# The MLP of layer 1 as seven products of quarters in place of eight

## The chip, the cores and the metric

The kernel runs on one core of a Trainium2 chip. The metric is the time of one execution in microseconds (us) of device time. Every time here is of the whole program, both layers, unless a stretch is named.

## The reference

The reference is one inference step of a decoder trunk of two layers: a gated linear attention (GLA) layer and a differential attention layer, each followed by a squared-ReLU MLP and a layer norm over a scaled residual. There are 1024 prompt tokens, 16 meta tokens ahead of them, and 8 sample tokens of running sequences. The model width is 1024, the MLP's inner width 4096; everything is float32.

```python
def sq_relu_mlp(x, w1, w2):          # w1 (1024, 4096), w2 (4096, 1024)
    h = jax.nn.relu(x @ w1)
    return (h * h) @ w2

def post_norm(x, f, g, b):
    return layer_norm(DEEPNORM_ALPHA * x + f, g, b)
...
    # in each layer, after the attention's own post_norm
    x_p = post_norm(x_p, sq_relu_mlp(x_p, mlp_w1[layer], mlp_w2[layer]), ln_mlp_g[layer], ln_mlp_b[layer])
    x_s = post_norm(x_s, sq_relu_mlp(x_s, mlp_w1[layer], mlp_w2[layer]), ln_mlp_g[layer], ln_mlp_b[layer])
```

The change concerns `sq_relu_mlp` for layer 1, the last work of the program.

## The kernel before

**Exact products from rounded parts.** TensorE multiplies in a rounded float32 format (fp32r). To keep float32's precision each operand is held as two parts: `hi`, the rounded value, which ScalarE (ACT) writes by a copy, and `lo`, what is left, source minus `hi`. `split` (L159 to L161) does this for activations, with VectorE (DVE) as the subtractor; `unit` (L138 to L154) does it for weights, with ACT at L151 and GpSimd (POOL) at L152. `mm3` (L163 to L166) then multiplies hi by hi, hi by lo and lo by hi, so every product of a 128 x 128 block is three matmuls, and all of them show lines 164 to 166 in the profile whatever stage they belong to.

**Storage.** Activations with features on the partitions lie in `XH` and `XL`, eight blocks of 128 features by 1032 tokens (1024 prompt, 8 sample). `Y` (seen as `Yt`, eight tiles of 128 tokens by 1024) holds the residual stream with tokens on the partitions and gathers the MLP's result. Three PSUM pools share the eight banks: `mm` with three tiles (`mmt`), `ax` with three (`axt`), `sm` with two (`smt`).

**The MLP of layer 1** (`mlp`, called at L1306) takes the 4096 inner features in eight groups of 512. In each group the up map goes first: two weight operands of 256 features (`kunit`), three chunks of 344 tokens, blocks of 128 features, eight blocks of the contraction, three matmuls each. ACT applies Relu (L946) and Square (L947) in PSUM, `split` writes the result to `HH` and `HL`. Then the down map: two weight operands of 512 outputs, eight tiles of 128 tokens, four blocks of the contraction, three matmuls of 512 columns each; DVE adds the PSUM tile into `Y` (L976). The sample tokens ride in the third chunk of the up map; their down map is a few small matmuls with the unsplit weights (L967), gathered in two PSUM tiles `acc` over the whole stage. In group 0, between the up and the down map, `alpha_row` scales the residual in `Y` (L924, DVE); the matching additions (L926) are spread over groups 1 to 4. Both read a row of a parameter that is broadcast from memory into `ht`.

**Ahead of it.** `w_out` (L840) is the attention's output projection, with 256-column matmuls; `normalize` takes each finished pair of token tiles through the layer norm's statistics (L880 to L894), and `to_fm` (L900) transposes a half of 512 tokens back to features on partitions and splits it into `XH` and `XL`. The last head of the attention, with `o_fm` (L1173 to L1179), writes the projection's input.

**Behind it.** In the last group the down map is ordered so that token tiles finish one after another; `normalize` and `last` (L1262 to L1279) turn a finished tile into output. Tiles 0 to 5 go over ACT (L894), DVE (L1269) and POOL (L1272), the last two over DVE alone (L1277, L1278). `samples_out` does the same for the sample tokens.

**What sets the order.** A scheduler places each engine's instructions in a fixed order at build time, from the order of the program and a simulated timeline; each engine then takes its own queue in order. A tile pool with n buffers lets the work of n tiles be under way; a new tile waits until the oldest is released. Nearly all loads are issued on the SP queue (`dma`).

## Time and profile before

| | |
|---|---|
| time, median of 3 runs | 2965.57 us (2965.27 to 2967.11) |
| the profiled execution: time, span of its instructions | 2961.38 us, 2959.4 us |
| mean granted TensorE clock | 0.988 |
| PE busy over the span | 2848.6 us (96%) |
| DVE, ACT, POOL busy over the span | 1579.2, 944.4, 836.6 us |

The profile is of one execution, a few microseconds from the median. Engines are PE (TensorE matmuls), PEld (its weight loads, which overlap the matmuls), DVE, ACT, POOL and SP. A group's row gives line, engine, operation, tiles out<-in, shapes, count | busy us, mean ns of one | idle time of the engine just before them, and what ended it. A row of a stretch gives its length, then for each engine busy us and instructions, the granted clock of PE, the busy share of the DMA engines and GB/s. A timeline row gives start, length, engine, line, operation, tiles, form and count. A row of waits gives who waited for whom: us in total, times, longest.

### The profile page before, as it was taken

The numbers are of one execution on the slowest core, as the hardware profiler recorded it, in microseconds if no ns is written. First come the engines' busy times: TensorE is split into PE (matmuls) and PEld (weight loads), VectorE is DVE, ScalarE is ACT, GpSimd is POOL, SyncE is SP. The second block draws the span as 40 slices with busy tenths as digits, with TensorE's granted clock in tenths as the row PEclk, the third lists the DMA queues.
The fourth block names the chain that finished last, engine by engine and source line by source line (L and its number), as shares of the span: only waits on it lengthen the run. The fifth ranks groups of instructions, "written<-read, shape, count | busy, mean of one in ns | idle before, by whom it ended". The sixth has DMA issues, their size and how long they took to land.

```text
span 2959.4 us, 50682 instructions
## 1 busy us (share of the span) xinstructions
PE 2848.6 (96%) x19476; PEld 2337.9 (79%) x19476; DVE 1579.2 (53%) x2705; ACT 944.4 (32%) x1970; POOL 836.6 (28%) x605
## 2 busy tenths in 40 slices
PE   8999999999999999999999998889999999999998
PEld 5776668987777777777888887878998889888886
DVE  2664454458877777777767623779352212211115
ACT  2343354152122122123311113768252232223322
POOL 1322022234333343344223320223312222222224
PEclk9999999999999999999999999999999999999999
DMA  8667541525798898988388987563412111111111
GB/s 262 208 206 260 181 153 52 174 86 165 254 349 305 292 334 315 338 309 301 114 282 293 360 311 193 109 139 91 168 35 61 45 40 34 57 44 50 38 34 65
DMA packets 266018, 525.81 MB, mean 178 GB/s; under 512 B 30560, under 2 KB 162656, under 8 KB 261680
## 3 DMA queue, kind: packets, MB, share of 16 engines
q1 hardware_dynamic: 260736, 505.97, 50.6%
q0 software_dynamic: 5040, 16.61, 2.9%
q8 instruction: 153, 2.51, 0.3%
q14 instruction: 89, 0.73, 0.1%
HBM read 479.78 MB, written 26.12 MB: 171 GB/s over the span
## 4 chain that ended last, share of the span: by engine, by line
PE 80%; DVE 8%; DMA 7%; ACT 2%; issue 1%; POOL 1%; SPq 1%; DVEq 0%; POOLq 0%; ACTq 0%
PE mmt L164 22%; PE mmt L166 22%; PE mmt L165 22%; PE smt L780 4%; DMA XL<-XL 1%; PE smt L1159 1%; DVE pg L739 1%; PE smt L967 1%; PE smt L418 1%; DVE as L1139 1%; DVE sc L740 1%; DMA swt<-in_mlp_w 1%; DMA XH<-XH 1%; DVE Y L924 1%; PE axt L1154 1%
## 5 line engine op out<-in xcount | busy, mean ns | idle before, releaser
L152 POOL TENSOR_TENSOR wlo<-raw,whi 128x512 fp32r<-128x512 f32 x384 | 528.7, 1392 | 1350.0 <-ACT whi L151 1195.5
L164 PE MATMUL mmt<-XH,whi 128*128 128x512 f32 (+1 forms) x1536 | 556.0, 362 | 8.8 <-DVE HL L161 8.8
L166 PE MATMUL mmt<-XH,wlo 128*128 128x512 f32 (+1 forms) x1536 | 555.3, 362 | 0.0
L165 PE MATMUL mmt<-XL,whi 128*128 128x512 f32 (+1 forms) x1536 | 554.1, 361 | 0.0
L151 ACT CAST whi<-raw 128x512 fp32r<-128x512 f32 x384 | 227.7, 619 | 932.4 <-PE mmt L166 475.8
L164 PE MATMUL mmt<-whi,XH 128*128 128x256 f32 x1536 | 439.0, 287 | 10.3 <-DVE qr L1028 5.2
L166 PE MATMUL mmt<-whi,XL 128*128 128x256 f32 x1536 | 438.6, 286 | 5.4 <-DVE XL L161 5.4
L165 PE MATMUL mmt<-wlo,XH 128*128 128x256 f32 x1536 | 436.6, 285 | 0.9 <-POOL wlo L152 0.8
L164 PE MATMUL mmt<-whi,HH 128*128 128x512 f32 x1024 | 411.3, 402 | 2.0 <-DVE Y L976 2.0
L166 PE MATMUL mmt<-whi,HL 128*128 128x512 f32 x1024 | 408.5, 399 | 0.0
L165 PE MATMUL mmt<-wlo,HH 128*128 128x512 f32 x1024 | 407.3, 398 | 0.0
L740 DVE TENSOR_REDUCE sc<-pg 128x16 f32<-128x1024 f32 x256 | 309.4, 1214 | 88.6 <-POOL pg L739 85.1
L976 DVE TENSOR_TENSOR Y<-Y,mmt 128x512 f32<-128x512 f32 x256 | 174.8, 684 | 317.6 <-PE mmt L166 317.2
L164 PEld LDWEIGHTS mmt<-XH,whi 128*128 128x128 f32 x1536 | 290.8, 189 | 48.9 <-DVE HL L161 10.4
L166 PEld LDWEIGHTS mmt<-XH,wlo 128*128 128x128 f32 x1536 | 290.8, 189 | 44.4 <-issue 12.0
L165 PEld LDWEIGHTS mmt<-XL,whi 128*128 128x128 f32 x1536 | 290.9, 189 | 41.3 <-issue 8.9
L164 PEld LDWEIGHTS mmt<-whi,XH 128*128 128x128 f32 x1536 | 291.0, 190 | 25.2 <-issue 17.7
L166 PEld LDWEIGHTS mmt<-whi,XL 128*128 128x128 f32 x1536 | 291.7, 190 | 16.8 <-issue 10.5
L165 PEld LDWEIGHTS mmt<-wlo,XH 128*128 128x128 f32 x1536 | 291.2, 190 | 11.5 <-issue 9.6
L739 DVE TENSOR_TENSOR pg<-pg,qb 128x1024 f32<-128x1024 f32 x192 | 263.2, 1376 | 64.7 <-DMA pg<-in_cache_k 46.7
L161 DVE TENSOR_TENSOR HL<-mmt,HH 128x344 fp32r<-128x344 f32 (+1 forms) x160 | 92.9, 582 | 327.2 <-ACT HH L160 327.0
L164 PEld LDWEIGHTS mmt<-whi,HH 128*128 128x128 f32 x1024 | 193.2, 189 | 73.5 <-DVE Y L976 17.5
(370 smaller groups left out, 3603.4 us busy)
## 6 DMA issues: line engine op xcount, KB each, us to landing
pg<-in_cache_k SPq DMA_DIRECT2D x256, 512.0 KB
pg<-in_cache_v SPq DMA_DIRECT2D x256, 512.0 KB
raw<-in_mlp_w SPq DMA_DIRECT2D x256, 256.0 KB
swt<-in_mlp_w SPq DMA_DIRECT2D x32, 1024.0 KB
raw<-in_gla_w_in SPq DMA_DIRECT2D x48, 256.0 KB
swt<-in_gla_w_in SPq DMA_DIRECT2D x12, 1024.0 KB
swt<-in_diff_w_in SPq DMA_DIRECT2D x12, 1024.0 KB
raw<-in_diff_w_in SPq DMA_DIRECT2D x48, 256.0 KB
```

Of the source, the lines that this page charges most:

```text
L151: S.copy(hi[:, c], raw)
L152: G.tensor_tensor(lo[:, c], raw, hi[:, c].bitcast(F32), op=ALU.subtract)
L161: return eng.tensor_tensor(lo, src, hi.bitcast(F32), op=ALU.subtract)
L164: TE.matmul(ps, ah, bh, start=first, stop=False)
L165: TE.matmul(ps, ah, bl, start=False, stop=False)
L166: TE.matmul(ps, al, bh, start=False, stop=last)
L418: TE.matmul(ps[o : o + TS, :], lhs[:, k + i, :], t[:, i, c * 512 : (c + 1) * 512], start=k == 0, stop=k == nk - 2)
L739: eng.tensor_tensor(pg, pg, qb, op=ALU.mult)
L740: return V.tensor_reduce(sc[:, n, :], pg.rearrange("p (h d) -> p h d", d=64), op=ALU.add, axis=AX.X).ins
L780: m = TE.matmul(acc[i * TS : i * TS + 16, :256], w[r, n, :], pg[r, i * 256 : (i + 1) * 256], start=n == 0, stop=n == NPG).ins
L924: steps_v.append(V.scalar_tensor_tensor(y, y, ALPHA, rb, ALU.mult, ALU.mult).ins)
L976: steps_v.append(V.tensor_tensor(yv, yv, ps, op=ALU.add).ins)
```

## The change

The up map and the down map of layer 1's MLP are each cut into 2 x 2 quarters, and the four quarters of the result come from seven products of quarters rather than eight, by a form of Strassen's identity with running sums. The 4096 inner features go in four runs of 1024, each with seven products for the up map (quarters of the weights: 512 x 512; of the activations: 512 features by 516 tokens, 512 prompt and 4 sample) and seven for the down map.

- `LEFT` and `RIGHT` say what each product multiplies: a quarter, a sum or difference of two quarters, or a quarter combined with the running operand `r` (kept in `RX` for activations, `RW` for weights).
- `chip_operand` makes the operand from activations: DVE combines (if there are two terms), ACT rounds, DVE subtracts, in two halves of two blocks. `weight_operand` makes the one from weights: four blocks of 128 x 512, one or two loads each, DVE combines, ACT rounds, POOL subtracts. Both are made one product ahead, and emitted in the middle of the product before.
- `up_tile` does 12 matmuls of 258 columns and adds the result into one or two quarters of `HF` (float32, in SBUF); `hidden` applies Relu and Square there when a quarter is complete. `down_tile` does 12 matmuls of 512 columns and adds into one or two quarters of `Y`, some of them by way of `RP` and an addition on POOL.
- The input of this MLP is kept unsplit (`xr`, in the place of `XL`), so `to_fm` no longer splits it.
- Around it: `XH` and `XL` become two tiles each, one for each half of the tokens; the PSUM pools become 4, 2 and 2 tiles ahead of this layer's output projection; the last head writes all eight blocks of the first half of the tokens before its own last tiles and the second half after; the last rows to finish are token tiles 0 to 3, of which 2 and 3 go over DVE alone. `mlp` now serves layer 0 alone.

The diff, cut to its core:

```diff
+LEFT = {1: [(0, 0)], 2: [(0, 1)], 3: [(0, 1), "-r"], 4: [(1, 1)], 5: [(1, 0), "+", (1, 1)], 6: ["r-", (0, 0)], 7: [(0, 0), "-", (1, 0)]}
+RIGHT = {1: [(0, 0)], 2: [(1, 0)], 3: [(1, 1)], 4: [(1, 0), "-r"], 5: [(0, 1), "-", (0, 0)], 6: [(1, 1), "-r"], 7: [(1, 1), "-", (0, 1)]}
...
-    XH = cp.tile([P, NB, 1032], F32R, name="XH")
-    XL = cp.tile([P, NB, 1032], F32R, name="XL")
+    TH = 512 + NS // 2
+    XH = Halves([cp.tile([P, NB, TH], F32R, name="XH%d" % c, tag="XH%d" % c) for c in range(2)])
+    XL = Halves([cp.tile([P, NB, TH], F32R, name="XL%d" % c, tag="XL%d" % c) for c in range(2)])
...
+    psum(mm=4, ax=2, sm=2)
...
-    normalize(w_out(A["diff_w_out"][0], True, samples()), stats, lambda c: to_fm(c, 2))
+    normalize(w_out(A["diff_w_out"][0], True, samples()), stats, lambda c: to_fm(c, 2, xr))
...
-    normalize(mlp(1, [(0, 344), (344, 688), (688, 1032)], hs, acc, rwp, mid=samples_out), stats, lambda c: None, last)
+    def chip_operand(terms, quarter, n, tmp):
+        buf = XH.t[count[0] % 2].rearrange("p k n -> p (k n)")
+        count[0] += 1
+        hi, lo = (buf[:, i * 4 * TH : i * 4 * TH + 4 * n].rearrange("p (k n) -> p k n", n=n) for i in range(2))
+        rv, tv = (x[:, : 4 * n].rearrange("p (k n) -> p k n", n=n) for x in (RX, tmp))
+        for j in (0, 2):
+            b = slice(j, j + 2)
+            src = combine(V, terms, lambda q: quarter(*q)[:, b], rv[:, b], tv[:, b])
+            split(hi[:, b], lo[:, b], src)
+        return hi, lo
+
+    def weight_operand(i, terms, quarter, side=None):
+        hi, lo = (wsp.tile([P, 2048], F32R, name=n).rearrange("p (k n) -> p k n", n=512) for n in ("whi", "wlo"))
+        for k in range(4):
+            raws = {}
+            for q in terms:
+                if isinstance(q, tuple):
+                    w, r0, c0 = quarter(*q)
+                    count[1] += 1
+                    raws[q] = wrp.tile([P, 512], F32, name="raw") if count[1] % 7 in (0, 3) else rawt()
+                    dma(raws[q], w[r0 + k * P : r0 + (k + 1) * P, c0 : c0 + 512])
+            run = RW[:, k, :]
+            src = combine(V, terms, raws.get, run, raws[terms[0]] if i == 7 else run)
+            S.copy(hi[:, k, :], src)
+            G.tensor_tensor(lo[:, k, :], src, hi[:, k, :].bitcast(F32), op=ALU.subtract)
+            if side:
+                side(k, raws)
+        return hi, lo
...
+    def hidden(h, c, m):
+        x = HF[:, 4 * h + m, c, :]
+        S.activation(x, x, AF.Relu)
+        S.activation(x, x, AF.Square)
+        S.copy(hs[:, 4 * h + m, 4 * c : 4 * c + 4], x[:, 512:])
+
+    def up_tile(g, i, m, c, left, right, ps):
...
+        for k in range(4):
+            mm3(ps, ah[:, k, ms], al[:, k, ms], bh[:, k, cs], bl[:, k, cs], k == 0, k == 3)
...
+        if i == 1:
+            S.copy(c12, ps)
+        elif i == 2:
+            add(c11, c12, ps)
+        elif i == 5:
+            S.copy(c22, ps)
+        elif i == 6:
+            add(c21, c12, ps)
+            add(c22, c22, c21)
+        elif i == 4:
+            add(c21, c21, ps)
+        elif i == 3:
+            add(c12, c22, ps)
+        else:
+            add(c22, c22, ps)
+            add(c21, c21, ps)
+        if c:
+            for h, x in {2: [(0, 0)], 3: [(0, 1)], 7: [(1, 1), (1, 0)]}.get(i, ()):
+                hidden(h, x, m)
+
+    DOWN = {1: [(0, 0)], 6: [(0, 1)], 7: [(1, 1), (1, 0)], 4: [(1, 0)], 5: [(1, 1), (0, 1)], 3: [(0, 1)], 2: [(0, 0)]}
+
+    def down_tile(g, i, t, left, right, ps):
...
+        r = RP[:, t, :]
+        if i == 1:
+            S.copy(r, ps)
+        if i in (6, 7):
+            add(V, r, ps)
+        for c, u in DOWN[i]:
+            yv = Yt[:, 4 * c + t, 512 * u : 512 * u + 512]
+            if i in (1, 2, 3, 4, 5):
+                add(V, yv, ps)
+            else:
+                add(G, yv, r)
+
+    def mlp1():
+        seq = []
+        for g in range(4):
+            seq += [(g, 1, i) for i in (1, 2, 5, 6, 4, 3, 7)]
+            seq += [(g, 0, i) for i in ((1, 5, 6, 3, 7, 4, 2) if g < 3 else (1, 5, 6, 7, 4, 3, 2))]
+        nxt = operands(*seq[0])
+        n = 0
+        for at, (g, up, i) in enumerate(seq):
+            now = nxt
...
+            for t in range(4):
+                if t == 2 and at + 1 < len(seq):
+                    nxt = operands(*seq[at + 1])
+                if up:
+                    for c in range(2):
+                        n += 1
+                        up_tile(g, i, t, c, *now, axt() if n % 3 == 0 else mmt())
+                    continue
+                n += 1
+                down_tile(g, i, t, *now, axt() if n % 3 == 0 else mmt())
...
+    normalize(mlp1(), stats, lambda c: None, last)
```

209 lines of the change are left out of this document (134 added, 75 removed).

## The prediction

> **What bounds the kernel now.** I read the page first, then a table of stretches, then the groups of the stage that changes, then the waits of PE, then the timeline where two engines meet. The page:
>
> ```profile
> span 2959.4 us, 50682 instructions
> PE 2848.6 (96%) x19476; PEld 2337.9 (79%) x19476; DVE 1579.2 (53%) x2705; ACT 944.4 (32%) x1970; POOL 836.6 (28%) x605
> PE   8999999999999999999999998889999999999998
> ...
> PE 80%; DVE 8%; DMA 7%; ACT 2%; issue 1%; POOL 1%; SPq 1%; DVEq 0%; POOLq 0%; ACTq 0%
> ```
>
> PE is busy nearly everywhere and carries four fifths of the chain that ended last. The MLP of layer 1 runs from about 2178 us to the end, so its ten slices of 74 us are the last ten of the page. Stretches with one form of matmul each (the MLP's loop in full in the last row):
>
> ```profile
> core 0: us, PE busy (x) PEld busy (x) DVE busy (x) ACT busy (x) POOL busy (x), PEclk, DMA share, GB/s
> 532.00:580.00 48.00, 48.00 (x407) 48.00 (x408) 21.41 (x31) 7.23 (x10) 13.76 (x10) 1.00 0.45 161
> 2380.00:2420.00 40.00, 40.00 (x257) 40.00 (x256) 5.68 (x11) 17.78 (x42) 7.63 (x6) 1.00 0.08 21
> 2449.00:2470.00 21.00, 21.00 (x91) 16.92 (x90) 6.05 (x8) 1.24 (x2) 3.95 (x4) 1.00 0.24 64
> 2600.00:2700.00 100.00, 100.00 (x532) 86.95 (x530) 18.23 (x30) 27.19 (x61) 20.37 (x16) 1.00 0.14 43
> ```
>
> In the stage PE is busy 100.00 of 100 us at the full granted clock, with DVE at 18%, ACT at 27% and POOL at 20%. Dividing each stretch by its count less two (matmuls that reach over the edges) gives the pitch of a matmul: 0.1185 us for 256 columns, 0.1569 for 344 (the up map), 0.2346 for 512 (the down map). The waits of PE from 2060 us to the end are few:
>
> ```profile
> PE mmt L164 <- DVE HL L161: 3.0, 1, 3.0
> PE mmt L164 <- DVE Y L858: 0.8, 1, 0.8
> PE mmt L164 <- ACT whi L151: 0.7, 1, 0.7
> PE axt L1177 <- DVE orr L1169: 0.4, 1, 0.4
> ```
>
> So nothing but PE limits this stage, and the change takes matmuls out of it and puts vector work in.
>
> **What PE loses.** The pitch grows nearly with the columns, so 258 columns cost 0.1185 x 258/256 = 0.1194 us (an estimate; no matmul of 258 columns is in this trace). Up map: before, 8 groups x 4 blocks x 3 chunks x 8 k x 3 = 2304 matmuls of 344 columns, 2304 x 0.1569 = 361.5 us; after, 4 runs x 7 products x 8 tiles x 4 k x 3 = 2688 of 258, 320.9 us. Down map: 8 x 16 tiles x 12 = 1536 of 512, 360.3 us; after 4 x 7 x 4 x 12 = 1344, 315.3 us. Together 721.8 - 636.2 = **86 us less**. The 64 matmuls of the samples' down map stay 64.
>
> **What the vector engines gain.** Each product now needs a left and a right operand made on the chip: a sum or a difference where the identity wants one, then a rounded high part (ACT) and a remainder (DVE for the activations, POOL for the weights). Its result must be added into up to two quarters. The prices, from the stage's groups (2220 to 2900 us; those behind the dots from 2176 us on):
>
> ```profile
> L152 POOL TENSOR_TENSOR wlo<-raw,whi 128x512 fp32r<-128x512 f32 x118 | 154.4, 1328 | 554.5 <-ACT whi L151 539.8 <-ACT hs L950 10.6 <-DMA raw<-in_mlp_w 3.7
> L976 DVE TENSOR_TENSOR Y<-Y,mmt 128x512 f32<-128x512 f32 x113 | 77.7, 688 | 248.5 <-PE mmt L166 248.5
> L151 ACT CAST whi<-raw 128x512 fp32r<-128x512 f32 x118 | 69.1, 617 | 338.0 <-PE mmt L166 260.0 <-DMA raw<-in_mlp_w 55.2 <-PE mmt L165 22.7
> L967 PE MATMUL smt<-raw,hs 128*32 128x512 f32 x118 | 31.6, 605 | 0.0
> L926 DVE SCALAR_TENSOR_TENSOR Y<-ht,Y 128x1024 f32<-128x1024 f32 x8 | 9.8, 1225 | 0.3
> L950 ACT COPY hs<-mmt 128x8 f32<-128x8 f32 x31 | 5.1, 166 | 9.3 <-DVE HL L161 9.3
> ...
> L894 ACT ACTIVATE Y<-Y,brs 128x1024 f32<-128x1024 f32 x10 | 12.0, 1238 | 17.4 <-DVE brs L892 17.4
> L880 DVE BATCH_NORM_STATS2 bst<-Y 128x6 f32<-128x512 f32 x18 | 12.2, 688 | 0.3
> L1269 DVE TENSOR_TENSOR Y<-Y,pg 128x1024 f32<-128x1024 f32 x6 | 8.0, 1326 | 0.0
> L1278 DVE SCALAR_TENSOR_TENSOR Y<-Y,brs,pg 128x512 f32<-128x512 f32 x4 | 2.8, 746 | 0.4 <-POOL brs L888 0.4
> L883 DVE BATCH_NORM_AGGREGATE bmv<-bst 128x2 f32<-128x12 f32 x10 | 2.0, 203 | 0.1
> L887 DVE TENSOR_SCALAR brs<-bmv 128x1 f32<-128x1 f32 x8 | 1.2, 149 | 0.2
> ```
>
> Durations of neighbours overlap a little, so for a queue of them I take the pitch, and for what POOL and DVE do to each other the timeline, DVE's rows first (two from 700 us, one from 245 us), then POOL's from 700 us:
>
> ```profile
> 700.30 13.57 DVE L739 TENSOR_TENSOR pg<-pg,qb 128x1024 f32<-128x1024 f32 x8
> 713.80 4.59 DVE L740 TENSOR_REDUCE sc<-pg 128x16 f32<-128x1024 f32 x4
> ...
> 245.56 1.28 DVE L320 TENSOR_TENSOR t<-gb 128x512 f32<-128x512 f32 x2
> ...
> 700.44 4.47 POOL L152 TENSOR_TENSOR wlo<-raw,whi 128x512 fp32r<-128x512 f32 x2 [5.03 <-ACT whi L151]
> 706.26 4.26 POOL L152 TENSOR_TENSOR wlo<-raw,whi 128x512 fp32r<-128x512 f32 x2 [1.34 <-ACT whi L151]
> ```
>
> Alone, 1024 elements pass DVE every 1.15 us (4.59/4) and 512 every 0.64. But eight L739, which read two tiles of SBUF, took 13.57 us where four POOL subtractions of L152 lay among them: 13.57 - 8 x 1.15 = 4.4, or **1.09 us of waiting per POOL instruction**, and POOL's took 2.2 us each in place of 1.3. The two take turns; they do not share. L976 and the present L161, which read one PSUM and one SBUF tile, show no such lengthening. All the new sums, differences and remainders on DVE read two SBUF tiles.
>
> The Trainium skill, "SBUF — State Buffer", section "Who interferes with whom", speaks against this change: a DVE instruction with two SBUF inputs and a GpSimd instruction that reads SBUF exclude each other for the whole instruction. The trace agrees in kind (L739 against L152), with 1.09 us measured where the whole POOL instruction is 1.3; by the rule to the letter the lock term below would be 41 us in place of 35, and the time 2930.
>
> Per run of 1024 features, up map: DVE 14 remainders and 8 combinations of 1032 elements at 1.16, 16 combinations of weights at 0.64, 56 evictions of 258 at 0.37 (from 512 at 0.64, by size, above nothing of fixed cost; an estimate): 25.5 + 10.2 + 20.7 = 56.4 us beside PE's 672 x 0.1194 = 80.2. Down map: 22 x 1.15 + 16 x 0.64 + 32 evictions x 0.64 = 56.0 beside 78.8 and 16 sample matmuls of 0.54 (31.6 us for 59, two records each), 8.6. POOL: 28 subtractions in each map, and 12 additions into Y in the down map: 68 a run. ACT: up 28 x 0.617 + 14 x 1.24 + 16 copies at some 0.35 + 16 x (2 x 0.617 + 0.166) = 62.7, down 37. Every sum is under PE's, so **on average all of it hides**. In single products it does not. An up product lasts 96 x 0.1194 = 11.5 us, a down product 11.3 (13 to 15 with sample matmuls), and in it DVE prepares the next operand pair and evicts its own. Making products 5, 6 or 7 takes 4 x 1.15 + 4 x 0.64 = 7.2; POOL's four subtractions, if each stops DVE, 4.4. Window by window, in the order of the list:
>
> - up 2 (it makes the operands of 5): 7.2 + 3.0 of evictions + 4.4 = 14.6, 3.1 over; up 3 (those of 7) the same; up 6 (those of 4): 4.6 + 5.9 + 4.4 = 14.9, 3.4 over; up 4 (those of 3): 4.9 + 3.0 + 4.4, 0.7 over; the others none;
> - down 5 (those of 6): 7.2 + 5.1 + 4.4 = 16.7 against 13.2, 3.5 over; down 3 (those of 7): 7.2 + 2.6 + 4.4 = 14.2, 2.9 over; down 6 (those of 3): 4.6 + 2.6 + 4.4, 0.3 over; the others none.
>
> That is 17 us a run if every POOL instruction stops DVE, 0 if none does (work made ahead in the light windows included): 67 or 0 over four runs. DVE's reads of two SBUF tiles fill (38.7 + 35.5)/167.6 = 44% of a run, so about half of POOL's starts meet one: **35 us**.
>
> **The rest.** The eight L924 and eight L926 for the residual were hidden; they are two-tile reads too and now fall among a busy DVE: 16 x 1.15 = 18 us at worst, 0 at best, half taken: 9. Behind a wait of L924 for its row stand, on DVE's queue, evictions and remainders. The switch from up 7 to down 5: ACT has 4.9 us of operands and 8 x 1.4 of Relu, Square and copy in an 11.5 us window, carries 4.6 over, and the chain combine, cast, remainder adds some 4 to it; down 1 lasts 15 and covers it; uncovered it would cost up to 5 a run. Weights go up from 128 loads (half of the row of both layers below) to 288 (the SP queue, seven buffers), 75 MB in 680 us, 111 GB/s; the table has 161 GB/s at full PE speed, so 0; behind a load that waits for a buffer stand the next loads alone, mostly. The start: the 3.0 us wait on HL L161 was for the second half of the tokens; now two products (23 us) run on the first half alone: -3. The first operand's cast and remainder lie beside the last two pieces of the output projection: 0, uncovered 5. The order of the last head's transposes and the wider PSUM pool: the one wait there is 0.4, so 0, between -3 and +3.
>
> ```profile
> raw<-in_mlp_w SPq DMA_DIRECT2D x256, 256.0 KB
> ...
> 2950.49 0.68 DVE L976 TENSOR_TENSOR Y<-Y,mmt 128x512 f32<-128x512 f32 x1
> 2953.58 1.41 DVE L1278 SCALAR_TENSOR_TENSOR Y<-Y,brs,pg 128x512 f32<-128x512 f32 x2
> ```
>
> The end: rows finish every 2.8 us in the last product rather than every 5.6, and DVE has 4 x (0.69 + 0.69 + 0.35) + 2 x 1.3 + 4 x 2 x 0.75 = 15.5 us of it, which begins when the first of four tiles is done and so ends 2.8 + 15.5 - 11.3 = 7.0 after the last matmul. Before, DVE ended 4.5 after it took up the last tile (2950.49 to 2954.99). +3, between 0 and 6.
>
> The sum: -86 - 3 + 35 + 9 + 3 = -42. The profiled execution took 2961.4 us (span 2959.4), so it would take 2919; the median of the three runs lies 4.2 above it at 2965.6, and on that scale the forecast is **2924 us**.
>
> **The rivals.** *All of it hides* (chance 0.18): the combinations are made ahead in the light windows and POOL falls between DVE's PSUM reads. For it: DVE's mean load of 112/168. Against: L739 and L152 met in turn whenever both had work. -86 - 3 + 3: 2880. *Operands come late* (0.20, the other side): engines take their queues in order, so an eviction that waits for PE stands ahead of a combination that PE's next product waits for. Then each of 55 products after the first starts late by one locked pair, 2.24 us (4.47/2): 123 - 86 + 9 = 46 slower, 3012. It decides against the change from 1.4 us a product on. For it: the locked pairs are real, and one operand is four links of combine, cast and subtract. Against: casts of L151 now start as soon as PE frees a buffer (260.0 us of their idle time ended so), so work is already ordered well ahead. *The smaller tile does not get cheaper* (0.03): were 258 columns to cost what 344 do, the up map would take 2688 x 0.1569 = 421.8, and 60 + 41 are lost: 101 - 42, 3025. The stretch at 532 us speaks against it. *In between* (0.09): late by 1.0 to 1.6 us a product, 2950 to 2985.
>
> **How the numbers follow.** The forecast, with overruns between 15 and 60 us, has 0.50. Range: from 2888, which leaves about half of the all-hidden case below, to 2985, which leaves the late case's upper part and the small-tile case above. A measurement of this kernel tells about 0.2%, 6 us, from no change. Faster by more: 0.50 + 0.18 + a little of the in-between, 0.71. Within: 0.05. Slower: 0.20 + 0.03 + the rest of the in-between, 0.24. The forecast's own range is 2900 to 2948.
>
> **What would show it.** Right: PE at 92 to 96% in the stage, DVE near 75 to 90%, POOL's L152 with a mean of 1.5 to 2.0 us, PE's waits led by DVE remainders and POOL's wlo at products 5, 6 and 7, a matmul of 258 columns at a pitch near 0.119. Wrong: PE at 99% (all hides); waits of equal size at every product (late operands); PE's waits led by ACT or by loads; a pitch over 0.13.

## The result, and the profile after

The change made the kernel slower: 2978.58 us (median; 2974.21 to 2986.99) against 2967.11 us before (2960.8 to 2975.4), measured on the same chip, a ratio of 1.0040 with a 95% interval of 1.0026 to 1.0055. I had forecast 2924, with 2888 to 2985 as the range: the time lies inside it, but the change went the other way than the one to which I gave 0.71, some 12 us slower by the ratio.

The profiled execution has a span of 2980.0 us, 20.6 more than before. The same lines of its page as were shown of before:

```profile
span 2980.0 us, 52275 instructions
PE 2799.5 (94%) x19668; PEld 2285.8 (77%) x19668; DVE 2013.0 (68%) x3122; ACT 1076.7 (36%) x2113; POOL 1147.2 (38%) x749
PE   8899999999999999999899998898998999999995
...
PE 25%; DVE 11%; DMA 5%; POOL 4%; issue 4%; ACT 1%; SPq 0%; DVEq 0%; POOLq 0%; ACTq 0%
```

PE is 49 us less busy in a longer span. The chain that ended last can't be set beside the one of before: followed back from the end it breaks off at 1476 us, so its shares add up to 50% where those of before add up to 99%. In the half that was followed PE has half, and VectorE, loads and GpSimd most of the rest. Stretches of the MLP (length, then busy us and instructions of PE, PEld, DVE, ACT, POOL, granted clock, DMA share, GB/s); the first row is the whole MLP before the change, the others are of after: the whole MLP, an up product 6 (18.4 us where 11.5 is undisturbed), a down product 7 (19.2 where 12.3 is), and the last product but one (33.6 where 11.1 is):

```profile
2178.00:2946.00 768.00, 765.00 (x4021) 660.06 (x4021) 191.78 (x314) 217.92 (x471) 184.36 (x153) 1.00 0.15 44
```

```profile
2201.00:2961.00 760.00, 699.04 (x4216) 603.12 (x4214) 626.30 (x733) 350.34 (x619) 485.34 (x292) 0.95 0.31 101
2436.10:2454.60 18.50, 14.21 (x99) 14.01 (x98) 16.65 (x18) 5.05 (x8) 8.50 (x5) 0.82 0.40 129
2538.30:2557.50 19.20, 16.10 (x57) 10.60 (x56) 14.75 (x14) 5.64 (x8) 16.79 (x11) 0.82 0.33 110
2913.50:2947.10 33.60, 15.38 (x67) 10.80 (x64) 25.12 (x45) 8.26 (x11) 25.88 (x26) 0.78 0.21 80
```

(Products are named by their map and number; runs 0 to 3 are the four runs of 1024 inner features.) Three things are to be seen. The MLP itself takes 760 us in place of 768: nearly all that PE was to save is gone. PE stands idle for 61 us of it (760.00 - 699.04; 3 before). And the granted clock has a mean of 0.95 where it was 1.00: with a clock of 1.0 or 0.5 that makes some 76 us at half speed. In the products that lost most both come together; up product 2 of run 0 (16.8 us) and up products 6 and 4 of run 3 (13.7 and 14.5) lost their 2 to 5 us at the full clock.

The 20.6 us by place, from the starts of the same matmuls in both traces: the first transposes of the attention come 2.4 earlier by chance (the instructions up to there are the same); from there to the MLP's first matmul 375.2 us in place of 349.6, so **25.5 more before the MLP begins** (five runs below leave the program unchanged up to there, and in them this stretch took 367.3 to 375.1 us, so single executions differ by some 8 us here); the MLP 8.4 less; from its last matmul to the end 18.8 in place of 13.0, 5.8 more.

In the MLP, each of the 56 products can be read off by its first matmul. Undisturbed they last 11.5 us (up), 11.1 (down), 14.35, 12.33 and 12.31 (down 1, 5 and 7, with sample matmuls), 656 in all; 104 us are lost, in four places of about equal size: up products 1, 2, 5, 6 and 4 of run 0 (25), down product 7 of every run (27), up products 6 and their neighbours in runs 1 to 3 (26), and the last two products of all (26). What PE waited for, from 2201 us to the end (in total, times, longest):

```profile
PE mmt L191 <- DVE HF L1414: 11.6, 8, 4.3
PE mmt L192 <- POOL wlo L1379: 9.9, 9, 2.0
PE smt L474 <- DVE ss L472: 7.7, 1, 7.7
PE mmt L192 <- DVE XH L188: 6.8, 2, 5.8
PE axt L191 <- DVE HF L1414: 5.9, 4, 2.9
PE smt L1333 <- DVE sx L487: 5.6, 1, 5.6
```

They are PSUM tiles that VectorE has not emptied (L1414), weight remainders of GpSimd (L1379), remainders of the activations that VectorE makes (L188), and the samples' small chain (L474, L1333), which no part of the prediction counted.

### The profile page after: what moved, and what is told of

Read it like the earlier page. It is cut to its first block, busy times and chain, and to the rows that moved or that the text cites. A ratio compares the mean times of both kernels' runs of the same rounds, so it can differ in the third digit from the quotient of the medians.

```text
span 2980.0 us, 52275 instructions
## 1 busy us (share of the span) xinstructions
PE 2799.5 (94%) x19668; PEld 2285.8 (77%) x19668; DVE 2013.0 (68%) x3122; ACT 1076.7 (36%) x2113; POOL 1147.2 (38%) x749
## 4 chain that ended last, share of the span: by engine, by line
PE 25%; DVE 11%; DMA 5%; POOL 4%; issue 4%; ACT 1%; SPq 0%; DVEq 0%; POOLq 0%; ACTq 0%
PE mmt L191 5%; PE mmt L193 5%; PE mmt L192 5%; DVE XH L188 2%; POOL wlo L1379 2%; DMA rw<-in_mlp_w 1%; POOL Y L1443 1%; PE smt L807 1%; PE smt L1177 1%; DMA XH<-XH 1%; PE axt L191 1%; DVE RW L1345 1%; DVE Y L1443 1%; PE axt L193 1%; DVE RX L1345 1%
## 5 line engine op out<-in xcount | busy, mean ns | idle before, releaser
L179 POOL TENSOR_TENSOR wlo<-raw,whi 128x512 fp32r<-128x512 f32 x256 | 364.9, 1439 | 777.3 <-ACT whi L178 688.9
L192 PE MATMUL mmt<-wlo,XH 128*128 128x256 f32 (+1 forms) x1824 | 557.3, 306 | 10.9 <-POOL wlo L1379 9.9
L191 PE MATMUL mmt<-whi,XH 128*128 128x256 f32 (+1 forms) x1824 | 558.2, 307 | 9.2 <-DVE qr L1047 4.0
L191 PE MATMUL mmt<-XH,whi 128*128 128x512 f32 (+1 forms) x1376 | 482.4, 352 | 19.7 <-DVE HF L1414 11.6
L191 PEld LDWEIGHTS mmt<-whi,XH 128*128 128x128 f32 x1824 | 349.0, 192 | 42.5 <-issue 18.6
L191 PEld LDWEIGHTS mmt<-XH,whi 128*128 128x128 f32 x1376 | 262.4, 191 | 62.2 <-DVE HF L1414 13.7
L192 PE MATMUL mmt<-XL,whi 128*128 128x512 f32 x768 | 306.8, 400 | 0.0
L766 POOL TENSOR_TENSOR pg<-pg,qb 128x1024 f32<-128x1024 f32 x64 | 156.9, 2452 | 308.7 <-DMA pg<-in_cache_k 224.2
L1379 POOL TENSOR_TENSOR wlo<-RW,whi 128x512 fp32r<-128x512 f32 x96 | 174.9, 1849 | 152.8 <-ACT whi L1378 148.1
L191 PE MATMUL mmt<-whi,HH 128*128 128x512 f32 x512 | 205.4, 401 | 1.9 <-DVE Y L991 1.9
L192 PE MATMUL mmt<-wlo,HH 128*128 128x512 f32 x512 | 204.5, 399 | 0.0
L193 PE MATMUL mmt<-whi,HL 128*128 128x512 f32 x512 | 203.8, 398 | 0.0
L192 PE MATMUL mmt<-XH,whi 128*128 128x258 f32 x608 | 175.5, 289 | 6.8 <-DVE XH L188 6.8
L1379 POOL TENSOR_TENSOR wlo<-rw,whi 128x512 fp32r<-128x512 f32 x88 | 152.1, 1744 | 75.5 <-ACT whi L1378 62.0
```

Of the source, the lines that this page charges most:

```text
L179: G.tensor_tensor(lo[:, c], raw, hi[:, c].bitcast(F32), op=ALU.subtract)
L191: TE.matmul(ps, ah, bh, start=first, stop=False)
L192: TE.matmul(ps, ah, bl, start=False, stop=False)
L193: TE.matmul(ps, al, bh, start=False, stop=last)
L766: eng.tensor_tensor(pg, pg, qb, op=ALU.mult)
L1379: G.tensor_tensor(lo[:, k, :], src, hi[:, k, :].bitcast(F32), op=ALU.subtract)
```

## The experiments

Ratios are to the kernel before, in runs on the same chip; the changed kernel's own is 1.0040. The intervals of the ratios are 3 to 9 us to either side, so a difference of two of them is known to some 5 to 10 us. An unchanged program varied by 13 to 22 us between its fastest and its slowest execution, so single profiles are compared by stretches, and totals by ratios. Every edit also lets the scheduler order the queues anew: in a run that alters the very end alone, up product 1 of runs 2 and 3 went from 13.9 and 13.3 us to 15.4 and 11.5. A difference of 2 us in one product tells little.

**PSUM pools opened once.** The change closes all PSUM pools behind the attention and opens them in other sizes.

```diff
-    psum(mm=4, ax=2, sm=2)
...
-                        up_tile(g, i, t, c, *now, axt() if n % 3 == 0 else mmt())
+                        up_tile(g, i, t, c, *now, axt() if n % 2 else mmt())
...
-                down_tile(g, i, t, *now, axt() if n % 3 == 0 else mmt())
+                down_tile(g, i, t, *now, axt() if n % 2 else mmt())
```

> PSUM pools are opened once (3, 3 and 2 tiles) and never closed; in the MLP the tiles alternate between the two rings of three. Theory: closing the pools makes w_out wait for the last PSUM tile of the attention; kept open, its first product runs among the transposes of the last head again (at about 2061 us, as before the change, not 2089), the MLP's first product begins near 2180 us instead of 2201, and the time falls by 18 to 25 us, to about 2957. Rival: it is the new order of o_fm (eight transposes of one half, then eight of the other) that holds w_out; then it begins at 2089 us still and the time stays within 5 us of 2979.

Measured: 0.9988 (0.9969 to 1.0007), some 15 us less than the changed kernel. The first matmul of `w_out` in the timeline (start, length, engine, line), of before, of after and of this run:

```profile
2061.22 0.36 PE L164 MATMUL mmt<-whi,XH 128*128 128x256 f32 x1
```

```profile
2089.34 0.58 PE L191 MATMUL mmt<-whi,XH 128*128 128x256 f32 x1 [1.17 <-DVE XL L1197]
```

```profile
2059.19 0.39 PE L191 MATMUL mmt<-whi,XH 128*128 128x256 f32 x1 [0.57 <-DVE ast L1157]
```

With the pools left open `w_out` fills the gaps of the last head again, as before. The way from the first transposes of the attention to the MLP fell from 375.2 to 362.4 us, 13 less, not the 18 to 25 expected, because `w_out` itself then takes longer, being shared with the head's rest (125.9 us from its start to the MLP, 111.9 in after). The edit also shares the tiles out otherwise in the MLP, but that took 760 us as in after, so the gain lies ahead of it.

**The closing alone, in the kernel before.**

```diff
+    psum(mm=3, ax=3, sm=2)
     e, hp, ht, HH, HL = open_mlp(T + NS)
```

> The kernel before the change, with its PSUM pools closed and opened again in their old sizes (3, 3, 2) ahead of w_out, and nothing else. Theory: the closing alone holds w_out until the last PSUM tile of the attention is free: its first product moves from about 2061 to about 2088 us, and the time rises by 10 to 16 us (in the run with the pools open the way from the first transposes of the attention to the MLP fell by 13 us). Rival: the closing only matters together with the new order of o_fm; then w_out begins by 2065 us and the time stays within 3 us.

Measured: 1.0000 (0.9983 to 1.0017). In its profile `w_out` begins at 2071.8 us, 10.6 later than before, between the theory's 2088 and the rival's 2065, and the MLP 8.7 later on the same path, which is about what single executions differ by there; the ratio shows no loss that can be told from none, and none above 5 us. So the closing alone does not explain the loss; that it costs its 13 us together with the new order of `o_fm`, whose eight transposes of the second half come in one piece at the end, fits both runs but is not shown: no run has the old order in the changed kernel.

**The samples' weights in rows.** Ahead of the MLP the samples pass the output projection in 32 narrow matmuls. The change loads their weights in quarter tiles of the small ring.

```diff
-        t = [rawt() for i in range(4)]
...
+        t = HF.rearrange("p k c n -> p (k c n)")[:, 1024 * k : 1024 * k + 2048].rearrange("p (k n) -> p k n", k=2)
+        for i in range(2):
+            dma(t[:, i, :], w[(k + i) * P : (k + i + 1) * P, :])
+        return t
```

> The changed kernel, but the weights of the samples' product ahead of the MLP are loaded in rows of 1024 into HF (empty by then), as pairs, not as quarter tiles of the ring of five. Theory: with quarter tiles each of the 32 narrow matmuls (128x32 by 512) waits for a load of its own and runs alone (0.43 us each, 12.6 us of TensorE), where before the change four ran side by side in 0.43 us (4.7 us for all); loaded in rows they run in fours again, the MLP begins about 8 us earlier and the time falls by 5 to 10 us, to about 2970. Rival: TensorE fills these waits with w_out anyway, so the time stays within 3 us of 2977.

Measured: 1.0002 (0.9987 to 1.0018), 11 us less than the changed kernel. The group's row under its tile, of after and of this run (duration least/median/most, first and last start):

```profile
L445 PE MATMUL smt<-rw,zoT x32: 592/592/617, 2119.5 to 2143.6; 128*32 128x512 f32 x32
```

```profile
L445 PE MATMUL smt<-HF,zoT x32: 592/592/617, 2111.0 to 2114.0; 128*32 128x512 f32 x32
```

In fours that write four different strips of the tile (32 partitions each), matmuls start 7 ns apart and the next four some 0.43 us later; one at a time each holds PE for 0.45 to 0.52 us. In after most ran one at a time, with weights in loads of their own and matmuls of `w_out` between them, 12.6 us of PE in place of 4.7 before and 3.6 in this run. The theory holds, and a little more than it was worth: the way from `w_out` to the MLP fell from 111.9 to 100.9 us, and 9 of these 11 us are the narrow matmuls' own.

**Scratch of its own for the samples' end.**

```diff
     def s2():
-        return rawt()
+        if own[0] is None:
+            return rawt()
+        own[0] += 1
+        return RX[:, 512 * (own[0] % 4) : 512 * (own[0] % 4) + 512]
```

> The five scratch tiles of samples_out lie in RX (dead by then) instead of in the ring of weight tiles. Theory: the raw tiles of the last product stand in the ring behind the scratch tiles, and these wait for the chain of the samples; with scratch of its own the last-but-one product (33.7 us) falls to between 11 and 15 us, the half clock behind it goes, and the time falls by 20 to 28 us, to about 2955. Rival: the chain of the samples itself (its steps on VectorE and ScalarE stand in front of the operands of the last product) holds TensorE; then the product keeps more than 25 us and the time falls by less than 8 us.

Measured: 0.9983 (0.9972 to 0.9994), 17 us less. ScalarE's timeline of after where PE stood still (in brackets the idle time ahead and its releaser):

```profile
2936.35 0.23 ACT L478 ACTIVATE sy__31801<-sv__31800 128x32 f32<-128x32 f32 x1 [8.41 <-DVE sv__31800 L477]
2942.74 0.57 ACT L1335 COPY rw<-smt 32x512 f32<-32x512 f32 x1 [5.90 <-PE smt L1333]
2943.59 0.57 ACT L1335 COPY rw<-smt 32x512 f32<-32x512 f32 x1 [0.28 <-PE smt L1333]
2946.46 0.62 ACT L1378 CAST whi<-rw 128x512 fp32r<-128x512 f32 x1 [2.30 <-DMA rw<-in_mlp_w]
```

The cast of the last product's weights (L1378) comes behind the samples' last copies into tiles of the same ring (L1335), and its load ended only then. With other scratch the last product but one fell from 33.7 to 18.4 us and the last from 14.1 to 12.5: two thirds of what it lost came from the ring. That is the theory's cause, but less than its size (11 to 15 us for the product, 20 to 28 for the time). Of the other 7 us above 11.1 PE waits 2.9 for the samples' chain on VectorE (L468), which is the rival's cause; the rest was not split further.

**RP's additions on VectorE.**

```diff
-                add(G, yv, r)
+                add(G if i == 7 else V, yv, r)
```

> The four additions of RP into Y of the sixth down product go from GpSimd to VectorE. Theory: they stand in GpSimd's queue among the weight subtractions of product 7; without them product 7 falls from 18.3-20.4 us to 13-14 us in each of the four runs, its half clock goes, and the time falls by 16 to 24 us, to about 2959. Rival: GpSimd and VectorE are both full there, so the place of the additions doesn't matter: VectorE becomes late in products 6 and 3 by as much (four additions of about 0.77 us a run, and what they lock out), and the time stays within 6 us of 2979 or rises.

Measured: 1.0029 (1.0012 to 1.0046), 3 us less than the changed kernel, within what can be told. Product 7 fell to 13.3, 13.5 and 13.2 us in runs 0 to 2, as expected, but kept 18.6 in run 3, whose order is another; product 2 rose from 11.1 to 18.9, 14.5 and 17.2. GpSimd's timeline of this run shows why:

```profile
2370.96 9.50 POOL L1443 TENSOR_TENSOR Y<-Y,RP 128x512 f32<-128x512 f32 x6
2380.41 1.27 POOL L1379 TENSOR_TENSOR wlo<-rw,whi 128x512 fp32r<-128x512 f32 x1
2381.64 3.47 POOL L1443 TENSOR_TENSOR Y<-Y,RP 128x512 f32<-128x512 f32 x2
2385.08 1.26 POOL L1379 TENSOR_TENSOR wlo<-raw,whi 128x512 fp32r<-128x512 f32 x1
```

Product 7's own eight additions now stand ahead of the remainders of product 2, which PE took up at 2380.0. The engine that came late was GpSimd again, not VectorE as the rival had it; the stall moved by two products.

**The residual not scaled.**

```diff
-                    with tc.issue_after(steps_v[-1]):
-                        list(alpha_row(A["ln_mix_g"][1:2], ALU.mult))
-                    beta = alpha_row(A["ln_mix_b"][1:2], ALU.add)
```

> Layer 1 leaves out the scaling of the residual (both alpha_row calls: 16 operations on VectorE and their loads). Theory: the eight multiplications stand in VectorE's queue before the operands and additions of products 2, 5, 6 and 4 of the first run (16.8, 18.0, 19.4 and 16.0 us); without them these four take 54 to 58 us together, as in runs 1 to 3 (56.5, 54.2 and 55.5), instead of 70.3, and the time falls by 12 to 17 us. Rival: the first run is slow because its operands are late from the layer norm just ahead (to_fm, half of it only then finished); then the four keep more than 66 us and the time falls by less than 5 us.

Measured: 0.9980 (0.9966 to 0.9993), 18 us less. Up products 2, 5, 6 and 4 of run 0 took 61.0 us in place of 70.3, between the theory's 54 to 58 and the rival's 66; the whole of run 0 11.7 less, the other three 7 less (where beta's additions were), so the theory's gain came, part of it elsewhere. The 61 us are still 6 to 8 above runs 1 and 2 of the same kernel (54.5 and 52.6), so run 0 has another cause beside it, which no run took apart.

**GpSimd out of the weights.** Low halves as copies by ScalarE:

```diff
-            G.tensor_tensor(lo[:, k, :], src, hi[:, k, :].bitcast(F32), op=ALU.subtract)
+            if free:
+                S.copy(lo[:, k, :], src)
+            else:
+                G.tensor_tensor(lo[:, k, :], src, hi[:, k, :].bitcast(F32), op=ALU.subtract)
```

> The low halves of the MLP's weights are second copies made by ScalarE instead of differences made by GpSimd (the differences are left out), but for the operands of the up product 6 and the down products 1 and 5, made while ScalarE is full. Theory: what GpSimd's subtractions cost is the port they share with VectorE (VectorE's remainder of 1024 columns takes 1.55-1.67 us where GpSimd is busy, 1.2 us alone) and their place in GpSimd's queue: VectorE's remainders fall to about 1.3 us, the up products 6 (19.4, 18.4, 16.2, 13.7 us) and the down products 7 (18.3-20.4) to under 14, and the time falls by 35 to 55 us, to about 2930. Rival: VectorE's own work is the limit in products 5, 6 and 4 (its queue is full with additions and the scaling of the residual), and ScalarE becomes late for the rest; then up product 6 keeps over 15 us in runs 0 and 1 and the time falls by less than 20 us.

Measured: 0.9791 (0.9761 to 0.9820), **74 us less** than the changed kernel. Runs 1 and 2 took 163.9 and 164.3 us (181.4 and 178.5): every up product 6 of runs 1 to 3 is at 11.49 and every down product 7 at 12.3. That is more than the theory asked for, and the rival falls, though up product 6 of run 0 still takes 15.8. But this run can't say whether the port or the waiting for GpSimd's results was the cost.

**The same, with GpSimd's work put back where nobody waits for it.**

```diff
             if free:
                 S.copy(lo[:, k, :], src)
+                G.tensor_tensor(spare, hi[:, k, :].bitcast(F32), hi[:, k, :].bitcast(F32), op=ALU.subtract)
```

> As the run with the low halves copied by ScalarE (2903 us; the differences are left out), but GpSimd still makes a difference of the same 128x512 operands for each copy, into a scratch tile (of two bytes an element) that nobody reads: its operations and what they lock are back, only no operand waits for them. Theory A, the port: VectorE's operations become slow again and the time returns to most of 2977, above 2950, with up product 6 at 15 us and more. Theory B, the lateness of GpSimd's results (1.8 us each, four a product, among its additions): the time stays below 2925, and up product 6 and down product 7 stay under 13.5 us in runs 1 and 2.

Measured: 0.9916 (0.9889 to 0.9943), 37 us above the run without and 37 below the changed kernel: neither theory alone. GpSimd's spare differences, and VectorE's remainders in after, without GpSimd's subtractions, and with them in vain, all from 2400 to 2850 us (busy, mean ns of one, idle before):

```profile
L1382 POOL TENSOR_TENSOR spare<-whi 128x512 bf16<-128x512 f32 x109 | 157.3, 1444 | 103.3 <-ACT whi L1379 97.6
```

```profile
L188 DVE TENSOR_TENSOR XH<-RX,XH 128x1032 fp32r<-128x1032 f32 x24 | 37.7, 1570 | 7.9 <-ACT XH L187 7.9
```

```profile
L188 DVE TENSOR_TENSOR XH<-RX,XH 128x1032 fp32r<-128x1032 f32 x21 | 29.1, 1387 | 5.3 <-ACT XH L187 5.3
```

```profile
L188 DVE TENSOR_TENSOR XH<-RX,XH 128x1032 fp32r<-128x1032 f32 x22 | 32.9, 1495 | 4.7 <-ACT XH L187 4.7
```

GpSimd's subtractions, with nobody waiting for them, bring the remainders from 1387 back to 1495 ns, more than half of the way to 1570, with up product 6 at 13.8, 12.9 and 11.6 us in runs 1 to 3 and down product 7 at 12.3 but for one of 14.6. That fits the port, and by this run it is worth some 37 us; what is left of the 74 goes with the waiting for GpSimd's results. The split is rough. The spare difference reads one tile twice and took 1.44 us on the mean, where those of after took 1.73 to 1.87. It also stands in GpSimd's queue ahead of RP's additions: VectorE waited 16.9 us for these in the MLP of this run, 5.8 without the spare differences and 9.6 in after, so the 37 us hold some of the queue too. And of the 31 us by which the MLPs of the two profiled executions differ, 8 lie in the last product but one (26.7 and 34.4 us), where the samples' end is. The Trainium skill, "SBUF — State Buffer", section "Who interferes with whom", has a DVE instruction with two SBUF inputs contend with a GpSimd instruction that reads SBUF; the rows agree in kind, with some 0.1 to 0.2 us more for a remainder.

**Stalls and the clock.** A kernel of matmuls alone, with standstills between blocks:

```diff
+        for k in range(170):
+            TE.matmul(ps, w, ys[i % 2], start=k == 0, stop=k == 169)
+        src = ps[:, :64]
+        for j in range(STALLS[i // 2] - 1):
+            V.tensor_scalar(ts[j % 2], src, 0.5, None, ALU.mult)
+            src = ts[j % 2]
+        S.activation(ys[(i + 1) % 2][:, :64], src, AF.Copy, scale=0.001)
```

> The whole computation is left out: 20 blocks of 170 matmuls (128x128 by 512, about 40 us each), each block waiting for a chain of small operations that begins when the block ahead ends, so that TensorE stands still for ten different lengths between about 1 and 10 us, each twice. Theory: a standstill of 1.5 to 2 us is already enough for the granted clock to fall to a half afterwards, for 3.4 us or a multiple (6.8, 10.2), so that a stall of 2 us costs 4 to 7 us; below about 1 us it costs only itself. Rival: the half clock belongs to longer lulls (TensorE thinly used over 10 us or more), and single stalls of up to 4 us between full blocks leave the clock at 1.0.

Its stretches, three pairs of a stall and what follows it:

```profile
523.10:526.50 3.40, 1.27 (x6) 0.77 (x5) 1.39 (x7) 0.26 (x1) 0.00 (x0) 1.00 0.00 0
526.50:529.90 3.40, 3.40 (x10) 2.62 (x9) 0.00 (x0) 0.00 (x0) 0.00 (x0) 0.50 0.00 0
...
564.10:567.50 3.40, 1.94 (x9) 1.28 (x7) 1.18 (x6) 0.00 (x0) 0.00 (x0) 1.00 0.00 0
567.50:570.90 3.40, 2.72 (x12) 2.27 (x13) 0.22 (x2) 0.26 (x1) 0.00 (x0) 1.00 0.02 5
...
649.40:652.80 3.40, 1.51 (x7) 0.94 (x5) 1.53 (x8) 0.00 (x0) 0.00 (x0) 1.00 0.00 0
652.80:656.20 3.40, 2.23 (x10) 1.85 (x11) 0.64 (x4) 0.26 (x1) 0.00 (x0) 1.00 0.00 0
```

PE's clock is granted for stretches of 3.4 us. Some 14 matmuls of 512 columns begin in a full one. The first pair's stretch, in which 4 begin (its row counts 6 with those that reach over the edges), is followed by one at 0.50; the other pairs', with 8 and 6, are not. Over the whole trace all stretches with 4 or fewer were followed by half clock, one of three with 6, and none with 7 or more; the only one with 5, itself at half clock, was followed by another at half. So the same standstill can do either: of two of 2.52 us between the starts of matmuls, one was followed by 3.4 us at half and the other, cut in two by the border, by none. All twelve of up to 2.06 us left the clock; one of 3.84 us halved it and one of 3.44 us did not; the two of 4.36 us halved it, one of 6.2 us for 6.8 us. The theory's 1.5 to 2 us was too low for a single stall, the rival's 4 too high. In after, three stalls of 1.64 us in a row at 2718.5 to 2722.9 us did it too. The Trainium skill, "TensorE: Matmul & The Clock Gate", section "HAM oscillation — how this bites in real kernels", warns of gaps over about 3.4 us; here 2.5 us in the wrong place is enough.

**Mended: x1, x2, x3.** The first puts the single findings together, with nothing left out of the computation:

```diff
-    psum(mm=4, ax=2, sm=2)
...
+            V.scalar_tensor_tensor(y, y, ALPHA, bc(row[:, 256 * j : 256 * j + 256], [P, 4, 256], 1), ALU.mult, ALU.mult)
+        to_fm(c, 2, xr)
...
-            G.tensor_tensor(lo[:, k, :], src, hi[:, k, :].bitcast(F32), op=ALU.subtract)
+            eng.tensor_tensor(lo[:, k, :], src, hi[:, k, :].bitcast(F32), op=ALU.subtract)
...
-                add(G, yv, r)
+                add(G if i == 7 else V, yv, r)
```

> The seven products with what the runs so far point to, nothing left out: PSUM pools opened once; the samples' weights loaded in rows into HF; scratch of samples_out in XF[0], called behind down product 7, run 3 in the order of the other runs; the scaling of the residual done as rows become ready ahead of to_fm (which divides by ALPHA), beta beside down products 4 and 2; RP's additions of product 6 on VectorE; the low halves for up 1 and 7 and down 4 and 2 made by VectorE, which is at 52-81% there; the last row's beta on VectorE for one tile. Theory: the parts add up as measured alone (-13, -18, -9, and about -32 for run 0 and product 7 together), so about 2905. Rival: VectorE is the common limit and what is taken from one product comes back in the next, as in the run with RP on VectorE; then over 2935.

Measured: 2928.59 us, 0.9857 (0.9827 to 0.9888), 54 us less than the changed kernel where 72 was the sum of the parts. Down product 7 is at 12.3 to 13.6 us and the end's 33.7 us are gone, but up product 1 of run 0 rose from 12.3 to 19.1 us, that of run 1 from 11.5 to 21.8, and the stretch behind the last matmul from 18.8 to 27.1. Theory and rival share it.

```diff
-            S.copy(c22, ps)
+            add(c22, c12, ps)
...
-            add(c22, c22, c21)
+            add(c22, c22, ps)
```

> As x1, but in the up products c22 gets its sum from PSUM twice (in product 5 c12 plus the tile, in product 6 plus the tile), so that product 6 has no addition of two SBUF tiles (0.77 us) and product 5 an addition more in place of ScalarE's copy. Theory: TensorE's waits in product 6 are for PSUM tiles that VectorE hasn't emptied; two additions of 0.41 us a tile instead of 0.41 and 0.77 bring product 6 to 11.5-12.5 us in runs 1 to 3 (13.7-18.4 before), and the time falls by 5 to 12 us against x1. Rival: the addition moved into product 5 fills VectorE there (98-105% busy), and the time stays within 3 us of x1.

Measured: 2913.12 us, 0.9834 (0.9803 to 0.9866), some 7 us less than x1, though the two intervals overlap. Not as expected: up product 6 kept 15.0 to 16.9 us in runs 1 to 3 (13.7 to 17.4 in x1); it was product 4 that fell, from 14.5 on the mean of four to 13.1.

```diff
+            if up and i == 3:
+                next(beta)
...
-            seq += [(g, 0, i) for i in (1, 5, 6, 3, 7, 4, 2)]
+            seq += [(g, 0, i) for i in ((1, 5, 6, 3, 7, 4, 2) if g < 3 else (1, 5, 6, 4, 7, 3, 2))]
```

> As x2, with the four steps of beta beside the up products 3 (VectorE at 57-77% there) instead of the down products 4 and 2, and the last run in the order 1, 5, 6, 4, 7, 3, 2, so that the rows 4 to 7 and the samples are complete two products before the end. Theory: the up products 1 of runs 1 and 2 (20.5 and 18.0 us) wait for low halves that stand behind beta in VectorE's queue, and the tail (27.1 us after the last matmul) is VectorE's work on all eight rows and the samples in a heap; so up product 1 falls under 13 us, the tail under 20 us, and the time to about 2892. Rival: VectorE is as full around up product 3, and product 4 or 6 takes over what product 1 loses; the tail alone gives some 6 us: about 2905.

Measured: 2904.51 us, **0.9805 (0.9780 to 0.9829)**, the best version: 58 us under the kernel before. Up product 1 of runs 1 and 2 is at 11.5 us, as the theory had it (run 0 keeps 19.5 and run 3 now has 15.4; down product 7 of run 1 has 17.8). The stretch behind the last matmul did not fall: 29.4 us, so that part was wrong; VectorE works on the rows almost without a gap for 24 us of it. The time is the rival's 2905, not the theory's 2892. The MLP of x3:

```profile
2170.00:2870.00 700.00, 674.57 (x4202) 588.06 (x4201) 630.84 (x812) 337.60 (x580) 350.57 (x201) 0.99 0.32 107
```

PE stands idle for 25 us of 700 in place of 61 of 760, at a clock of 0.99. VectorE is as busy as in after (631 us to 626), in a stage 60 us shorter. So a kernel with seven products can be 2% faster than the one before. What x1 to x3 changed beside the products (the early scaling of the residual, for one) was not tried in the kernel before, so not all of the gain need be the products' own.

## Why the prediction was wrong, point by point

**PE's saving: right.** An up product lasts 11.49 us undisturbed, 0.1197 us a matmul where I estimated 0.1194; a down product 11.1, 0.231 where I took 0.2346. 28 of each kind make 89 us saved; I had 86. The whole stage had more to give: its products undisturbed add up to 656 us where the MLP before took 768, 112 less. Of the other 23 us the samples' matmuls give 8 (23 us in place of 31), and the one stall of before with its half clock some 5; the rest was not taken apart.

**The overruns: the mechanism right, the sum over windows the step that failed.** The signs named came: GpSimd's remainders at 1.73 to 1.87 us (1.5 to 2.0 named), VectorE at 82%, PE's waits led by VectorE and by GpSimd's wlo, mostly at products 5, 6 and 7. Two of these rows, from 2400 to 2850 us:

```profile
L1379 POOL TENSOR_TENSOR wlo<-RW,whi 128x512 fp32r<-128x512 f32 x60 | 110.3, 1867 | 99.0 <-ACT whi L1378 99.0
L1379 POOL TENSOR_TENSOR wlo<-rw,whi 128x512 fp32r<-128x512 f32 x56 | 96.1, 1732 | 35.3 <-ACT whi L1378 35.3
```

But 35 us for the lock (67 at the most; my own 44% of it would have been 30) and 9 for the residual's rows, 44 us, was all that the MLP was to lose, and it lost 104; without most of GpSimd's subtractions the kernel was 74 us faster. The 37 us that came back with the subtractions in vain are near the term of 35, but that is in part luck: of the windows that I named as over, up 3 and down 5 (3.1 and 3.5 us) lost next to nothing in all four runs, nor did the products behind them, while up product 6 and down product 7 lost up to 8 us. The other half, operands that wait in GpSimd's queue, had no term. Two things were not in the sum, and the runs showed a third.

First, I summed the durations in each window and let PE lose only what stuck out at its end. The engines' queues have an order: GpSimd's twelve additions of RP a run, which I counted in its load alone, stand ahead of subtractions that the next product waits for. Run 0's down product 7 in after, GpSimd's rows and the first of PE's:

```profile
2354.93 2.21 POOL L1443 TENSOR_TENSOR Y<-Y,RP 128x512 f32<-128x512 f32 x1 [1.76 <-DVE RP L1443]
2357.09 1.72 POOL L1379 TENSOR_TENSOR wlo<-raw,whi 128x512 fp32r<-128x512 f32 x1
2358.77 2.25 POOL L1379 TENSOR_TENSOR wlo<-rw,whi 128x512 fp32r<-128x512 f32 x1
...
2358.86 0.62 PE L192 MATMUL mmt<-wlo,XH 128*128 128x512 f32 x1 [2.03 <-POOL wlo L1379]
```

The addition waits for VectorE, the remainder behind it for the addition, and PE, which took up this product at 2355.7 us, for the remainder. In the up products PE also stops inside a product when its PSUM tiles (there are six) wait for VectorE.

Second, a stall has a second price. I gave no term to the clock, though the trace of before held one case, a stall of 3.3 us at 2207.8 us with half clock after it:

```profile
2207.50:2210.90 3.40, 0.65 (x5) 0.35 (x3) 2.59 (x3) 2.75 (x8) 0.00 (x0) 1.00 0.03 9
2210.90:2214.30 3.40, 3.15 (x11) 3.15 (x12) 1.76 (x4) 0.00 (x0) 0.00 (x0) 0.50 0.13 39
```

In after some 76 us of the MLP run at half, in ten spells, which is up to 38 us lost. Six of the spells follow a single stall of 2.3 to 6.1 us (from start to start of the matmuls), the longest one of 8.1.

Third, relief by moving a cause is partial: taking the additions off GpSimd freed product 7 and stopped product 2.

**The residual's rows: too small.** 9 us, at most 18; leaving them out gave 18, the whole of the bound, half of it in up products 5 and 6 of run 0.

**"The order of the last head's transposes and the wider PSUM pool: 0, between -3 and +3": wrong.** It cost 13 us on this path (15 by the ratio). I went by the one wait in the trace of before (0.4 us) and not by what the lines do: closing a pool lets no new tile be had until every old one is free, which takes from `w_out` the gaps of the last head that it filled before (2061 us).

**"The SP queue, seven buffers: 0": wrong.** The bandwidth was right (101 GB/s in the MLP; I had 111). What I left out is who else draws on the ring of weight tiles: the samples' product ahead of the MLP, whose weights come in quarter tiles (11 us), and the samples' scratch at its end (17 us).

**The tail: +3, between 0 and 6; measured 5.8.** The end of VectorE's work waits for GpSimd there, whose eight additions of 8.26 us stand ahead of the last row's power:

```profile
2965.20 8.26 POOL L1304 TENSOR_TENSOR Y<-Y,XR 128x256 f32<-128x256 f32 x8 [2.13 <-DVE Y L1301]
2973.42 0.55 POOL L909 TENSOR_TENSOR brs<-brs,mhalf 128x1 f32<-128x1 f32 x1
```

**The switch from up 7 to down 5, and the start.** Down product 1 covers the switch as said (14.35 us in all four runs). The 3.0 us of the start may have been won, but they can't be seen beside the 25 us that run 0 loses.

**The rivals.** The time lies towards "operands come late", and 104 us over 55 products are 1.9 each, above the 1.4 from which it was to decide. But it is not that mechanism in its even form: more than half of the products lose nothing, and the 104 us lie in four places with different causes. From -42 to +20.6 it is 63 us in the profiled executions (by the ratio, +12, it is 54): 37 in the MLP (-8.4 where the terms gave -45), 23 ahead of it (25.5, less the 2.4 by chance; the pools' 13 and the samples' weights' 11 account for it), and 3 in the tail. The 37 are a net figure: the losses were 60 above the 44 priced, and the 23 us that the stage had to give beyond the terms of 86 and 3 hide that much of them. The single findings overlap and can't be added up: 74, 18 and 17 us would be more than the 104 lost.

What stays open: how the 13 us ahead of the MLP divide between the closing of the pools and the new order of the transposes; how GpSimd's 74 us divide between port and queue, beyond a rough half; what else slows run 0; and how much of the 76 us at half clock would stay lost were PE not also waiting in them.

## What to carry to other kernels

Where a change swaps matmuls for vector work, price the new work by its place in each engine's queue, not by sums over a window: an operand is late by whatever stands ahead of it, and a stall of PE that empties a clock stretch is paid a second time at half speed. Read a diff for what it does to shared things (a pool that is closed, a ring that a second user draws on) even where the trace shows no wait there, since a wait that isn't there yet has no row. And test a suspected engine by taking its work out and then putting it back with nobody waiting: the two runs together part contention from lateness, as far as the work put back is the same and stands in nobody's way.

## What the hardware showed that I had not expected

The granted clock follows PE's activity in stretches of 3.4 us: in the kernel of matmuls alone, 4 starts of the some 14 that a full stretch holds were followed by half clock, 7 were not, and 6 once in three times. So one stall of 2.5 us costs nothing or 1.7 us more by where it falls. Matmuls of 32 output rows in different strips of a PSUM tile start 7 ns apart, four in some 0.43 us; issued one at a time each cost 0.45 to 0.52 us, which nothing in a sum by counts shows.
